# State-space layer: the stores of the turned outputs issued by ScalarE instead of SyncE

## Chip, core and metric

One NeuronCore of a Trainium2 chip runs the whole program. The metric is the device time of one execution in microseconds. TensorE (PE) multiplies matrices, VectorE (DVE), ScalarE (ACT) and GpSimd (POOL) work on tiles, and SyncE (SP) issues transfers. Each engine takes its instructions in the order in which they stand in its own queue, and semaphores tie the engines together. A DMA that an engine issues is an instruction of that queue; the transfer itself runs on 16 DMA engines.

## What is computed

A trunk of two layers over 1024 positions of width 1024, in float32. The first layer mixes attention and a short convolution, the second is a state-space layer, and each is followed by a gated feed-forward network. The change lies in the state-space layer:

```python
def s5_mixer(h, w_in, lambda_re, lambda_im, log_step, b_re, b_im, c_re, c_im, d_skip, w_glu):
    u = (h @ w_in).astype(f32)
    ug = u.reshape(bsz, seq, SSM_GROUPS, SSM_GROUP)        # 64 groups of 16 channels
    ...
    _, _, st_r, st_i = lax.associative_scan(_ssm_combine, (a_r, a_i, bu_r, bu_i), axis=1)
    y = (einsum("gcp,bsgp->bsgc", c_re, st_r) - einsum("gcp,bsgp->bsgc", c_im, st_i)).reshape(...)
    y = y + d_skip * u
    g = jax.nn.gelu(y)
    a, b = jnp.split(g @ w_glu, 2, axis=-1)
    return a * jax.nn.sigmoid(b)
```

## The kernel before

Activations lie with channels on the partitions. Every large matrix product splits both factors in a high and a low part (`wh`, `wl`; `g_h`, `g_l`) and adds three products (`mm_unit`, L169). ScalarE makes the high part of a weight, GpSimd the low part (`split_w`, L150); for G, ScalarE makes the high part and VectorE the low part (`split_g`, L1344).

The state-space layer works in eight blocks m of 128 channels, which are eight groups of 16. Positions are taken as 128 chunks of 8. A block passes through these stages, each a function that is named in the table `order` (L1399):

- U `unit` (L1365): the input product on TensorE. W `weights` splits its weights. E `enter` evicts it as `u`.
- X `store_inputs` (L1249) stores `u` to memory (`ud`), and T `turn_inputs` (L1252) loads it with eight DMAs as `ut`, where a partition holds a position in its chunk and a channel, and the free axis the groups and chunks. The turn is done by way of memory.
- S_ `states` (L1277), one per block, here called step m: `px` on TensorE (L1288), a copy `xs` on ScalarE (L1293, L1294), products and a scan on VectorE (`sc`, L1303), a copy `ss` on ScalarE (L1306, L1307), and `sp` on VectorE. C `copy_rotations` (L1269) copies the rotation table `cs` on ScalarE ahead of it. The step then loads the tables `et` and `cs` of the next one.
- O `emit` (L1318): `py` on TensorE, and GELU on ScalarE into `gy` (L1330). There is one `gy` buffer for blocks 0 to 6; block 7 has another. It then loads the tables `tt` and `co` of the next block.
- R `turn_outputs` (L1334): eight DMAs (L1337) of 16 partitions and 64 KB each store `gy` to `gd`, turned back. F `fetch` loads a block of `gd` as `graw` (L1341), and Q `place` splits it into `g_h` and `g_l`.
- G `gated`: the first three units of the product with `w_glu`, in parts, as blocks of G come in.

All this is recorded under `tc.manual_schedule()` (L1409): the instructions stand in each engine's queue in the order of the table. For the change it matters what stands next to R there:

```python
(C, 1), (S_, 1), (T, 3), (U, 5, 0), (O, 0), (X, 4), (R, 0), (W, 6), (C, 2), (S_, 2), ...
(C, 4), (S_, 4), (R, 2), (F, 1), (X, 6), (C, 5), (S_, 5), ...
(S_, 7), (F, 4), (G, 1, 2, 3), (R, 5), (G, 0, 3, 4), (O, 6), (G, 1, 3, 4), (R, 6), (F, 5), (Q, 4), ...
```

Each DMA counts on one of eight semaphores, and one that uses a semaphore again waits until the transfer that used it last has landed. Before the change all DMAs of the kernel are issued by SyncE. After the stretch the rest of the product with `w_glu`, the second feed-forward network and its last product run.

Of the kernel before, what the change touches and what calls it, by code (L numbers as in the profile page):

```python
# [39 lines left out]
GC = 16  # L40
# [10 lines left out]
def hybrid_trunk_kernel(ctx: ExitStack, tc: tile.TileContext, xt, gains, mix_w_in, w_uq, w_ukv, q_gain, k_gain,  # L51
                        mix_w_out, ssm_w_in, lambda_re, lambda_im, log_step, b_re, b_im, c_re, c_im, d_skip, w_glu,
                        ffn_w_up, ffn_w_down, rope_cos, rope_sin, causal, eye16, halves, out, dbg=None):
    nc = tc.nc
# [216 lines left out]
    for gr in range(2):  # L271
        gts = []
        for i in range(2):
            m = 2 * gr + i
# [959 lines left out]
    gd = dp.tile([KT, P, L, NCH], F32, name="gd")  # L1234
    with ExitStack() as p5s:
# [98 lines left out]
        def turn_outputs(m):  # L1334
            gy = gys.pop(m)
            for j in range(L):
                nc.sync.dma_start(out=gd[m, :, j, :].rearrange("(g c) n -> c g n", c=GC), in_=gy[GC * j:GC * j + GC])  # L1337

        def load_g(m):
            t = wh_tile("graw", F32)  # L1340
# [51 lines left out]
        def place(m):  # L1392
            split_g(m, graw.pop(m))

        pg = []
        U, E, X, T, S_, O, R, W = (unit, into, store_inputs, turn_inputs, step_states, step_outputs, turn_outputs,
                                   weights)
        G, F, Q, C = gated, fetch, place, copy_rotations
# [474 lines left out]
```

## Time and profile before

| | |
|---|---|
| median of 3 runs | 2347.11 us (2344.19 to 2349.64) |
| the profiled execution's own time | 2344.66 us |
| its span | 2342.9 us |
| busy: PE, DVE, ACT, POOL | 2248.5, 1614.7, 851.3, 767.0 us |
| mean granted TensorE clock | 0.986 |
| DMA: one queue, issued by SP | 26.9% of 16 engines' span |
| stores of `gy` | 64 issues of 64 KB, 1370.5 to 1483.1 us, 3.0 us to landing in the median |

The span is the time between the first and the last instruction of the one execution that was profiled. A row of an order of time gives the start, the duration, and in brackets how long the engine was idle before it and whose end ended that. Issues of DMAs do not count as busy time. SPq and ACTq are the queues of SyncE and ScalarE, with their DMA issues and semaphore instructions.

### The profile page before, as it was taken

The page shows a single profiled execution, that of the slowest core. Times are in us where ns is not written, and L with a number is a line of the kernel's source. Part 1 is how long each engine was busy: PE and PEld are TensorE (multiplying, and loading weights), DVE is VectorE, ACT ScalarE, POOL GpSimd, SP SyncE. Part 2 cuts the span into 40 slices and gives each one's busy share as a digit, 9 for nine tenths or more (in the row PEclk, how much of TensorE's full clock was granted, in tenths as well). Part 3 has the DMA queues.
Part 4 walks back from the last instruction along what each step waited for, and adds up shares of the span by engine and source line. Part 5 has one row for each costly group of instructions (what it writes and reads, how often), then busy time and mean ns, then how long its engine had stood idle before and what let it go on. Part 6 is the DMA issues. An engine that isn't in the chain of part 4 may idle for free.

```text
span 2342.9 us, 29810 instructions
## 1 busy us (share of the span) xinstructions
PE 2248.5 (96%) x11228; PEld 1867.9 (80%) x11228; DVE 1614.7 (69%) x2650; ACT 851.3 (36%) x1446; POOL 767.0 (33%) x575
## 2 busy tenths in 40 slices
PE   7999899999999999999999988999789999999999
PEld 6888888888788878888888877788568888878887
DVE  6344677787978778879777487323888888876542
ACT  4112566664232333332223255312444444443110
POOL 4322454435233222232224344431043333324220
PEclk9999999999999999999999998999999999999999
DMA  4112000012122221223332288521132222245301
GB/s 155 45 38 57 1 10 10 10 46 72 29 66 62 82 68 49 76 80 92 101 102 63 93 223 242 171 72 41 54 110 93 82 81 81 81 153 181 125 10 72
DMA packets 227152, 192.04 MB, mean 82 GB/s; under 512 B 25472, under 2 KB 202944, under 8 KB 227008
## 3 DMA queue, kind: packets, MB, share of 16 engines
q1 hardware_dynamic: 227008, 190.14, 26.9%
q8 instruction: 88, 1.44, 0.2%
q14 instruction: 56, 0.46, 0.1%
HBM read 148.22 MB, written 46.07 MB: 83 GB/s over the span
## 4 chain that ended last, share of the span: by engine, by line
PE 79%; DVE 11%; issue 3%; DMA 3%; ACT 3%; POOL 1%; SPq 0%; DVEq 0%; POOLq 0%; ACTq 0%
PE pu L175 31%; PE pd L190 22%; PE pc L1648 4%; PE pb L1648 4%; PE pa L1648 4%; PE pd L1648 2%; PE pu L1554 1%; PE pss L586 1%; PE po L634 1%; PE pckv L378 1%; PE pq L446 1%; PE ptp L615 1%; DVE xT L1696 1%; PE pcq L378 1%; PE pda L644 1%
## 5 line engine op out<-in xcount | busy, mean ns | idle before, releaser
L154 POOL TENSOR_TENSOR wl<-raw,wh 128x1024 fp32r<-128x1024 f32 (+2 forms) x115 | 289.1, 2515 | 487.3 <-ACT wh L153 242.3
L193 DVE TENSOR_TENSOR xT<-pd,xT 128x512 f32<-128x512 f32 x320 | 204.3, 682 | 160.4 <-PE pd L190 159.8
L153 ACT ACTIVATE wh<-raw 128x1024 fp32r<-128x1024 f32 (+2 forms) x117 | 122.4, 1051 | 305.8 <-PE pu L175 212.6
L175 PE MATMUL pu<-f_h,wh 128*128 128x512 f32 x704 | 219.4, 393 | 0.0
L175 PE MATMUL pu<-f_l,wh 128*128 128x512 f32 x704 | 217.2, 390 | 0.0
L175 PE MATMUL pu<-f_h,wl 128*128 128x512 f32 x704 | 216.7, 389 | 0.0
L175 PEld LDWEIGHTS pu<-f_l,wh 128*128 128x128 f32 x704 | 132.1, 188 | 27.9
L175 PEld LDWEIGHTS pu<-f_h,wl 128*128 128x128 f32 x704 | 132.1, 188 | 27.9
L175 PEld LDWEIGHTS pu<-f_h,wh 128*128 128x128 f32 x704 | 130.7, 188 | 28.7 <-issue 1.7
L810 POOL TENSOR_TENSOR gl<-c,gh 128x512 fp32r<-128x512 f32 x44 | 61.4, 1415 | 247.0 <-ACT gh L809 247.0
L1696 DVE SCALAR_TENSOR_TENSOR xT<-u,vec,xT 128x1024 f32<-128x1024 f32 x84 | 111.1, 1330 | 13.3 <-ACT xT L1694 12.6
L759 DVE TENSOR_TENSOR u<-pu,f_rb 128x512 f32<-128x512 f32 x88 | 56.8, 685 | 89.9 <-PE pu L175 87.9
L190 PE MATMUL pd<-gh,wh 128*128 128x512 f32 x352 | 113.5, 403 | 5.4 <-DVE u L759 2.9
L190 PE MATMUL pd<-gh,dwh 128*128 128x512 f32 x352 | 108.8, 390 | 2.5 <-DVE xT L193 1.5
L190 PE MATMUL pd<-gl,wh 128*128 128x512 f32 x352 | 110.4, 395 | 0.0
L190 PE MATMUL pd<-gh,wl 128*128 128x512 f32 x352 | 110.0, 394 | 0.0
L190 PE MATMUL pd<-gh,dwl 128*128 128x512 f32 x352 | 108.5, 389 | 0.0
L190 PE MATMUL pd<-gl,dwh 128*128 128x512 f32 x352 | 108.4, 389 | 0.0
L1796 POOL TENSOR_TENSOR dwl<-raw,dwh 128x1024 fp32r<-128x1024 f32 x20 | 60.8, 3066 | 112.5 <-PE pd L190 84.3
L761 ACT ACTIVATE c<-u,vec 128x512 f32<-128x512 f32 x88 | 59.9, 717 | 69.5 <-DVE u L759 69.1
L190 PEld LDWEIGHTS pd<-gh,wh 128*128 128x128 f32 x352 | 65.8, 191 | 22.6 <-DVE xT L193 4.0
L190 PEld LDWEIGHTS pd<-gh,dwh 128*128 128x128 f32 x352 | 66.1, 188 | 16.9 <-DVE xT L193 1.9
(569 smaller groups left out, 5790.6 us busy)
## 6 DMA issues: line engine op xcount, KB each, us to landing
raw<-in_ffn_w_up_dram SPq DMA_DIRECT2D x50, 512.0 KB, 3.8
raw<-in_ffn_w_down_dram SPq DMA_DIRECT2D x42, 512.0 KB, 4.4
xT<-in_ffn_w_up_dram SPq DMA_DIRECT2D x40, 512.0 KB, 3.6
gfd<-xT SPq DMA_DIRECT2D x21, 512.0 KB, 2.6
raw<-gfd SPq DMA_DIRECT2D x20, 512.0 KB, 4.0
raw<-in_w_glu_dram SPq DMA_DIRECT2D x16, 512.0 KB, 4.0
raw<-in_mix_w_in_dram SPq DMA_DIRECT2D x14, 512.0 KB, 3.9
xT<-in_xt_dram SPq DMA_DIRECT2D x8, 512.0 KB, 7.6
```

The source lines that it names most:

```text
L153: nc.scalar.activation(h[:, 0:n], raw[:, 0:n], AF.Copy)
L154: eng.tensor_tensor(out=l[:, 0:n], in0=raw[:, 0:n], in1=h[:, 0:n].bitcast(F32), op=ALU.subtract)
L175: nc.tensor.matmul(ps[hf], lhsT=w[wi][:, P * k:P * k + P], rhs=xs[k][xi][:, HALVES[hf]], start=(k == 0 and wi == 0 and xi == 0), stop=(k = ...
L190: nc.tensor.matmul(ps[hf], lhsT=ws[i][wi][:, P * f:P * f + P], rhs=gts[i][xi][:, HALVES[hf]], start=(i == first and wi == 0 and xi == 0), ...
L193: nc.vector.tensor_tensor(out=xT[f][:, HALVES[hf]], in0=ps[hf], in1=xT[f][:, HALVES[hf]], op=ALU.add)
L378: nc.tensor.matmul(ps[:, HALF * j:HALF * j + n], lhsT=xa[k][xi][:, P * (2 * p + j):P * (2 * p + j) + P], rhs=w[k // kw][wi][:, n * (k % kw ...
L759: nc.vector.tensor_tensor(out=u[:, 2:HALF + 2], in0=ps[hf], in1=rb[:, HALVES[hf]], op=ALU.mult)
L761: nc.scalar.activation(c, u[:, 2:HALF + 2], AF.Copy, scale=cwcol(layer, 2, m))
L810: nc.gpsimd.tensor_tensor(out=gl[:, cols], in0=cv[hf], in1=gh[:, cols].bitcast(F32), op=ALU.subtract)
L1648: nc.tensor.matmul(ps, lhsT=w[:, HALF * wi + P * k:HALF * wi + P * k + P], rhs=x.at(xi, k), start=(start and k == 0 and wi == 0 and xi == ...
L1696: nc.vector.scalar_tensor_tensor(out=c, in0=u[:, w:S + w], scalar=cwcol(self.layer, w, m), in1=c, op0=ALU.mult, op1=ALU.add)
L1796: eng.tensor_tensor(out=l, in0=raw, in1=h.bitcast(F32), op=ALU.subtract)
```

## The change

`turn_outputs` issues its eight DMAs from ScalarE. Nothing else of the source differs.

```diff
         def turn_outputs(m):
             gy = gys.pop(m)
             for j in range(L):
-                nc.sync.dma_start(out=gd[m, :, j, :].rearrange("(g c) n -> c g n", c=GC), in_=gy[GC * j:GC * j + GC])
+                nc.scalar.dma_start(out=gd[m, :, j, :].rearrange("(g c) n -> c g n", c=GC), in_=gy[GC * j:GC * j + GC])
```

ScalarE's queue at two places: behind `gy` of block 0, and from the second `ss` of step 7 to `g_h` of block 4 and on. `g_h_13966`, `g_h_14013` and `g_h_14023` are `g_h` of blocks 4, 5 and 6.

```order
 L1330 ACT_TABLE_LOAD
 L1330 ACTIVATE gy<-py 128x512 x2
+L1337 DMA gd<-gy 16x8x128 x8
 L153 ACTIVATE wh<-raw 128x1024
 L1269 ACTIVATE cs<-cs 64x2048
```

```order
 L1306 ACTIVATE ss<-sc 64x512
 L1307 ACTIVATE ss<-sc 64x512
+L1337 DMA gd<-gy 16x8x128 x8
 L1330 ACTIVATE gy<-py 128x512 x2
+L1337 DMA gd<-gy 16x8x128 x8
 L1346 ACTIVATE g_h_13966<-graw 128x1024
 L1330 ACTIVATE gy<-py 128x512 x2
+L1337 DMA gd<-gy 16x8x128 x8
 L1346 ACTIVATE g_h_14013<-graw 128x1024
 L1346 ACTIVATE g_h_14023<-graw 128x1024
```

The eight issues stand ahead of `wh` and `cs` at the first place, and ahead of `gy`, `g_h` of block 4 and `g_h` of block 5 at the second. The same instructions leave SyncE's queue.

ScalarE's queue of the changed kernel around R(1), with the semaphores that each instruction waits for (DMAHW0 to DMAHW7 are those of the transfers, and every row's name ends in one number that is the same for all):

```order
L1330 ACTIVATE gy_13238<-py_13249 128x512 [waits PE_49]
L1337 DMA gd_12586<-gy_13238 16x8x128 [waits DMAHW6_49,Activation_49]
L1337 DMA gd_12586<-gy_13238 16x8x128 [waits DMAHW7_49]
L1337 DMA gd_12586<-gy_13238 16x8x128 [waits DMAHW1_49]
L1337 DMA gd_12586<-gy_13238 16x8x128 [waits DMAHW3_49]
L1337 DMA gd_12586<-gy_13238 16x8x128 [waits DMAHW5_49]
L1337 DMA gd_12586<-gy_13238 16x8x128 [waits DMAHW7_49]
L1337 DMA gd_12586<-gy_13238 16x8x128 [waits DMAHW1_49]
L1337 DMA gd_12586<-gy_13238 16x8x128 [waits DMAHW3_49]
L153 ACTIVATE wh_13298<-raw_13146 128x1024
```

On SyncE the eight semaphores were used in turn. Now the two queues share them, and within R(1) numbers 7, 1 and 3 come twice, four issues apart. In R(0) the third issue waits for DMAHW1, on which the load of `co` just ahead of it counts. The first `gy` of block 6, behind R(5), waits for the transfers of R(5):

```order
L1337 DMA gd_12586<-gy_13803 16x8x128 [waits DMAHW4_49]
L1330 ACTIVATE gy_13925<-py_13926 128x512 [waits DMAHW3_49,DMAHW4_49,DMAHW2_49,DMAHW6_49,DMAHW1_49,DMAHW7_49,DMAHW0_49,PE_49]
L1330 ACTIVATE gy_13925<-py_13936 128x512 [waits PE_49]
```

TensorE's queue differs at one place, where the last block of G (`g_h7`) comes in: matmuls of the next unit with blocks 0 and 1 stood ahead of those with block 7, and now stand behind them.

```order
-L175 MATMUL pu_14137<-g_h0_13634,wh_14133 128x512
-L175 MATMUL pu_14138<-g_h0_13634,wh_14133 128x512
-L175 MATMUL pu_14137<-g_l0_13635,wh_14133 128x512
-L175 MATMUL pu_14138<-g_l0_13635,wh_14133 128x512
-L175 MATMUL pu_14137<-g_h0_13634,wl_14134 128x512
-L175 MATMUL pu_14138<-g_h0_13634,wl_14134 128x512
-L175 MATMUL pu_14137<-g_h1_13638,wh_14133 128x512
 L175 MATMUL pu_13691<-g_h7_14059,wh_13579 128x512
 L175 MATMUL pu_13692<-g_h7_14059,wh_13579 128x512
-L175 MATMUL pu_14138<-g_h1_13638,wh_14133 128x512
-L175 MATMUL pu_14137<-g_l1_13639,wh_14133 128x512
-L175 MATMUL pu_14138<-g_l1_13639,wh_14133 128x512
```

Ten matmuls move in this way. VectorE's queue is the same.

## Rows read from the trace of the kernel before

**Rows 1.** The page: chain that ended last, shares of the span by engine.
```profile
PE 79%; DVE 11%; issue 3%; DMA 3%; ACT 3%; POOL 1%; SPq 0%; DVEq 0%; POOLq 0%; ACTq 0%
```

**Rows 2.** Busy time of PE, PEld, DVE, ACT, POOL; granted clock, DMA share, GB/s.
```profile
1340.00:1495.00 155.00, 130.53 (x717) 112.28 (x716) 106.33 (x162) 78.76 (x105) 63.76 (x40) 0.91 0.82 230
...
1495.00:1620.00 125.00, 125.00 (x553) 103.46 (x553) 32.98 (x24) 27.68 (x40) 43.02 (x22) 1.00 0.23 72
```

**Rows 3.** Order of time, PE: start, us, instruction, idle before it and its releaser.
```profile
1371.50 1.20 PE L175 MATMUL pu<-s_h,wh 128*128 128x512 f32 x2 [5.01 <-ACT wh L153]
...
1411.88 3.75 PE L1288 MATMUL px<-ut,et 128*128 128x128 f32 x16 [9.38 <-DMA gd<-gy]
...
1469.91 0.73 PE L175 MATMUL pu<-g_h,wh 128*128 128x512 f32 x2 [3.40 <-ACT g_h L1346]
...
1483.22 0.62 PE L175 MATMUL pu<-g_h,wh 128*128 128x512 f32 x2
...
1492.30 0.97 PE L175 MATMUL pu<-g_h,wh 128*128 128x512 f32 x3 [0.54 <-ACT g_h L1346]
```

**Rows 4.** Order of time, ACT, from the first `gy` to the end of the stretch.
```profile
1369.42 1.08 ACT L1330 ACTIVATE gy<-py 128x512 f32<-128x512 f32 x2
...
1390.83 0.59 ACT L1293 ACTIVATE xs<-px 64x512 f32<-64x512 f32 x1 [2.86 <-PE px L1288]
...
1412.85 0.63 ACT L1306 ACTIVATE ss<-sc 64x512 f32<-64x512 f32 x1 [1.80 <-DVE sc L1303]
...
1427.09 1.07 ACT L1330 ACTIVATE gy<-py 128x512 f32<-128x512 f32 x2
...
1432.50 1.06 ACT L153 ACTIVATE wh<-raw 128x1024 fp32r<-128x1024 f32 x1 [2.45 <-DVE g_l L1347]
1436.58 1.06 ACT L1346 ACTIVATE g_h<-graw 128x1024 fp32r<-128x1024 f32 x1 [3.02 <-DMA graw<-gd]
1437.54 1.07 ACT L1330 ACTIVATE gy<-py 128x512 f32<-128x512 f32 x2
...
1455.74 1.92 ACT L1269 ACTIVATE cs<-cs 64x2048 f32<-64x2048 f32 x1 [1.59 <-DMA cs<-csd]
...
1467.83 1.09 ACT L1330 ACTIVATE gy<-py 128x512 f32<-128x512 f32 x2
1468.80 1.06 ACT L1346 ACTIVATE g_h<-graw 128x1024 fp32r<-128x1024 f32 x1
...
1479.81 2.00 ACT L1346 ACTIVATE g_h<-graw 128x1024 fp32r<-128x1024 f32 x2
```

**Rows 5.** Order of time, SP; then all issues of L1337: ns min/median/max.
```profile
1367.07 0.38 SPq L1274 DMA_DIRECT2D co<-cpd  x1
...
1370.53 3.66 SPq L1337 DMA_DIRECT2D gd<-gy  x8
...
L1337 SPq DMA_DIRECT2D gd<-gy x64: 302/428/997, 1370.5 to 1483.1; - x64
```

**Rows 6.** Issues to landing (us): R(0), R(6), `co` (1367.07), `et` of steps 5, 7.
```profile
gd<-gy SPq DMA_DIRECT2D x8, 64.0 KB, 2.8
...
gd<-gy SPq DMA_DIRECT2D x8, 64.0 KB, 2.1
...
co<-cpd SPq DMA_DIRECT2D x1, 512.0 KB, 5.4
...
et<-etd SPq DMA_DIRECT2D x1, 512.0 KB, 8.8
...
et<-etd SPq DMA_DIRECT2D x1, 512.0 KB, 4.1
```

**Rows 7.** The chain in order of time around the second `ss` of step 7.
```profile
1466.47 0.02 ACTq L1306
1466.49 0.04 issue
1466.53 0.09 ACT ss L1306
1466.62 0.04 issue
1466.66 0.04 ACTq L1330
```

## The prediction

> **What bounds the kernel now.** I read the chain of work first, then the busy time of the stretch around the change, then each engine's order of time there. TensorE carries the chain [rows 1]. The 64 moved stores all lie in the state-space stretch. There TensorE is busy for 130.53 of 155 us, ScalarE for 78.76 [rows 2]. From 1495 to 1620 us TensorE is busy for 125.00 of 125 us [rows 2], and nothing there can take back lost time: what TensorE loses in the stretch, the kernel loses. Inside it TensorE has four long waits: 5.01 us for the weights `wh`, 9.38 before step 5's `px`, 3.40 for `g_h` and 0.54 for the last `g_h` [rows 3]. Three of the four end on an instruction of ScalarE, so I look at what stands ahead of those in ScalarE's queue.
>
> **What moves.** I call the eight stores of channel block m R(m). On SyncE eight unhindered issues take 3.66 us (median of all 64: 428 ns) [rows 5]. SyncE loses all 64, or 64 × 0.428 = 27.4 us of issuing; ScalarE gains them. No row shows a DMA issued by ScalarE. The nearest row is the same store on SyncE, and I take it: 3.7 us for a group. Bounds: 0.04 us for one, as ScalarE's queue takes for a semaphore instruction [rows 7], and 1.0 us, the slowest of the 64 [rows 5].
>
> A group is dear where ScalarE has work behind it. Three things hang on it:
> - The issue itself: each group follows `gy` or a step's `ss`, and the next `wh`, `cs`, `xs` or `g_h` stands behind all eight.
> - A semaphore is used again within R(1) after four issues, as the rows of the order show, and so in R(2) to R(4). Landing takes 2.8 us (median of R(0)'s eight) [rows 6], four issues 4 × 0.46 = 1.9, so 0.9 us more.
> - There is one `gy` buffer, and O(m) waits for R(m-1) to land. That binds where R(m-1) stands just ahead of O(m).
>
> **Does ScalarE issue past a waiting `ss`?** The second `ss` of step 7 waits for VectorE's scan. The semaphore instructions of the `gy` behind it run at 1466.66 us, after the wait was released at 1466.47, not in the 1.8 us before [rows 7]. The queue is held at that wait, and R(2) and R(5), which stand behind such an `ss`, begin at the release; only the two `ss` (1.3 us) lie beside them. The Trainium skill ("Perfetto Trace Analysis", the section on VectorE and ScalarE instructions) says that the sequencer fetches on once an instruction is in the wait queue; by that alone both groups would issue earlier, under the scan, and the sum would be 13.2 us instead of 21.0 (second rival). The row speaks against it here.
>
> **The sum**, as the delay of ScalarE's chain, which TensorE meets at the `g_h` it waits for:
> 1. R(0), between `gy` (ends 1370.50) and the `wh` that TensorE already waits for [rows 3, 4]: 3.7. Its third issue uses the semaphore of `co`, which was issued at 1367.07 and took 5.4 us [rows 5, 6]: to 1372.5 instead of 1371.5, 1.0. Delay 4.7.
> 2. R(1): 3.7 + 0.9, less the 2.86 us that ScalarE waits for step 3's `px` [rows 4]; `px` itself is late by term 1, so that wait stays. +1.7, delay 6.4.
> 3. R(2): 3.7 + 0.9, less the 1.3 beside the two `ss` after 1412.85 [rows 4]. +3.3, delay 9.7. TensorE's wait before step 5 is set by `et`, which lands 8.8 us after its issue [rows 6]; it moves by 4.7 only, so ScalarE is the later one.
> 4. R(3) follows block 3's `gy` (ends 1428.16 [rows 4], now 1437.9). The 4.6 us to 1442.5 lie beside two `g_h` and the 2.45 us wait before `wh`, and the 3.02 us wait for `graw` is swallowed. But `gy` of block 4 must wait for R(3) to land: 1442.5 + 2.8 = 1445.3, against 1437.54 before [rows 4]. Delay now 7.8.
> 5. R(4), ahead of `wh` and step 6's `cs` and `xs`: 3.7 + 0.9. Delay 12.4.
> 6. `cs` of step 7 was late by 1.59 us [rows 4]; this wait is swallowed. Delay 10.8.
> 7. R(5) starts at the release (1466.53 [rows 7]). Eight issues 3.7, landing 2.1 (R(6)'s median [rows 6]), and only then `gy` of block 6, which started at 1467.83 [rows 4]: 3.7 + 2.1 - 1.3 = 4.5. Delay 15.3.
> 8. R(6), between that `gy` and `g_h` of block 4 (1468.80), for which TensorE waits [rows 3, 4]: 3.7. Delay 19.0.
> 9. R(7) moves `g_h` of blocks 5 and 6 (1479.81 [rows 4]) back by 3.7. TensorE first reads block 5 at 1483.22 [rows 3], 2.4 us after it is there: 1.3 exposed. The last `g_h` comes no earlier, so these 1.3 us end in the gap that ten filling matmuls fill now; the order puts those behind it, and they still have to run: 10 × 0.226 us (553 in 125.00 us [rows 2]) = 2.3, of which the 0.54 us wait gives some back. +2.0, delay 21.0.
>
> Together 21.0 us. SyncE's gain is priced at nothing beyond the waits swallowed in 4 and 6, since its loads mostly wait for TensorE to free a single buffer (`et`, `tt`, `co`). The half clock that follows TensorE's stalls is left at nothing: the stalls are there already. The profiled execution took 2344.66 us, 2.45 under the median of the runs (2347.11). 2344.66 + 21.0 = 2365.7, from the median 2368.1; I give **2366**.
>
> **Rivals.**
> - *SyncE's relief decides, and it is faster.* Place: loads behind R(2) to R(4) on SyncE. ScalarE is idle for 76 of 155 us [rows 2], room for eight groups of 3.7. If they fell into it, what is left is the gain: the 3.02 and 1.59 us waits of ScalarE for loads [rows 4], and of TensorE's 9.38 us as much as `et` takes too long (8.8 against 4.1 for a later one, 4.7 [rows 6]): 9.3 us, 2335.4. It decides if the groups expose less than 9.3 us. Against it: `et` stands ahead of R(2) in its queue already, and where R(6) comes to stand, `gy` and `g_h` now follow each other without a gap [rows 4]. The Trainium skill ("DMA: Bandwidth & Descriptors", the section on issuing engines) says that issuing from several engines saves only sequencer time, which takes from this rival the `et` part, leaving 2340.0. Chance 0.05.
> - *ScalarE's queue runs past waiting instructions.* Terms 3 and 7 fall away: delay 6.4, at block 4's `gy` 4.5 by its landing, 9.1 after R(4), 7.5, 11.2 after R(6), 13.2: 2357.9. Against it rows 7. Chance 0.14.
> - *An issue is almost free on ScalarE.* At 0.08 us with its gap a group is 0.6 us, but semaphores and landings remain: R(0) 2.3 (to the landing of `co`), R(1) 0.2, R(2) 1.8, at block 4's `gy` 1.4 in all, R(4) 3.1, `cs` -1.6, R(5) 1.4, R(6) 0.6: 4.9 us, 2349.6, on the edge of what counts as the same. Chance 0.10.
> - *An issue is dearer there.* At 0.8 us a group takes 6.7. Then the semaphores come free by themselves, and the same walk gives 7.0, 10.8, 16.2, 16.3, 23.0, 21.4, 29.0, 35.7, 40.1: 2385. For it: 997 ns in rows 5, and two engines issuing at once. Chance 0.14.
> - *Nothing is seen*, because TensorE waits elsewhere as long. Against it: its waits end on ScalarE. 2345, chance 0.02.
>
> **How the numbers follow.** The forecast has 0.55. It and the run-ahead rival lie in 2352 to 2381, with most of the dear one; almost free, nothing and faster lie below, the worst of dear above: about 0.8 inside. 0.2% is 4.7 us, about what a measurement of this kernel can tell from no change. Slower: 0.55 + 0.14 + 0.14 + half of the almost free case, 0.88. Same: the other half and the nothing case, 0.07. Faster 0.05.
>
> **What would show it.** Step by step: L1337 on ScalarE's queue at about 0.43 us each; `wh` behind R(0) late by about 4.7 us and TensorE's 5.01 us wait near 9; `xs` of step 5 some 10 us late; R(5) directly after the release and `gy` of block 6 after its landing; a TensorE wait of about 10 us for `g_h` of block 4, where there were 3.40. After it TensorE is busy throughout, some 21 us later. The forecast is wrong if an issue costs under 0.1 us, if R(2) and R(5) run during the scan, or if step 5's `px` comes early enough to pay for the rest.

## The result and the profile after

The changed kernel takes 2372.02 us (median of 5 runs, 2370.10 to 2373.57), the kernel before 2347.11 us (5 runs beside them): ratio 1.0107, 95% interval 1.0094 to 1.0121, **24.9 us slower**. The forecast was 2366 us, with a range of 2352 to 2381. The profiled execution of the changed kernel is the slowest of its five (2373.57 us, span 2371.8), so between the two traces the difference is 28.9 us.

The page of the changed kernel, its chain by engine and its two large DMA queues (packets, MB, share of 16 engines' span):

```profile
PE 78%; DVE 11%; issue 3%; ACT 3%; DMA 3%; POOL 2%; ACTq 0%; SPq 0%; DVEq 0%; POOLq 0%
...
q1 hardware_dynamic: 217792, 185.94, 25.8%
q10 hardware_dynamic: 9216, 4.20, 0.7%
```

TensorE carries the chain as before [rows 1], and the stores now have a queue of their own. The busy time by stretch of the changed kernel, with the columns of [rows 2]:

```profile
1340.00:1522.00 182.00, 134.99 (x708) 115.30 (x707) 106.50 (x162) 80.80 (x107) 65.30 (x40) 0.83 0.70 196
1522.00:1647.00 125.00, 125.00 (x553) 103.52 (x552) 30.67 (x23) 25.74 (x38) 40.90 (x21) 1.00 0.22 70
```

The stretch that took 155 us takes 182, with nearly the same counts of instructions on every engine. After it TensorE is busy throughout, as before: nothing is taken back. The granted clock of the stretch fell from 0.91 to 0.83, that is, more of it ran at 1.2 instead of 2.4 GHz, and TensorE's busy time rose by 4.46 us (130.53 to 134.99).

The issues of L1337 (ns min/median/max) in the changed kernel:

```profile
L1337 ACTq DMA_DIRECT2D gd<-gy x64: 309/442/2027, 1370.6 to 1509.3; - x64
```

An issue costs ScalarE 442 ns in the median, about what it cost SyncE, 428 [rows 5]. Its order of time on TensorE, with the columns of [rows 3]:

```profile
1375.51 1.22 PE L175 MATMUL pu<-s_h,wh 128*128 128x512 f32 x2 [8.91 <-ACT wh L153]
...
1422.40 3.75 PE L1288 MATMUL px<-ut,et 128*128 128x128 f32 x16 [11.21 <-DMA cs<-csd]
...
1498.33 1.22 PE L175 MATMUL pu<-g_h,wh 128*128 128x512 f32 x2 [12.98 <-ACT g_h L1346]
...
1510.87 0.74 PE L175 MATMUL pu<-g_h,wh 128*128 128x512 f32 x2 [1.42 <-ACT g_h L1346]
```

The waits of 5.01, 9.38 and 3.40 us [rows 3] are now 8.91, 11.21 and 12.98. The last row is a wait that was not there before: 1.42 us for `g_h` of block 5, which stands behind R(7). The wait of 0.54 us for the last `g_h` is gone. Why the waits grew stands in ScalarE's order of time:

```profile
1370.61 3.74 ACTq L1337 DMA_DIRECT2D gd<-gy  x8
1374.40 1.06 ACT L153 ACTIVATE wh<-raw 128x1024 fp32r<-128x1024 f32 x1 [3.82 <-DMA gd<-gy]
...
1389.08 4.77 ACTq L1337 DMA_DIRECT2D gd<-gy  x8
...
1396.90 0.59 ACT L1293 ACTIVATE xs<-px 64x512 f32<-64x512 f32 x1
...
1410.68 1.91 ACT L1269 ACTIVATE cs<-cs 64x2048 f32<-64x2048 f32 x1 [2.52 <-DMA cs<-csd]
...
1421.41 0.63 ACT L1306 ACTIVATE ss<-sc 64x512 f32<-64x512 f32 x1 [1.74 <-DVE sc L1303]
1421.46 0.79 ACTq L1337 DMA_DIRECT2D gd<-gy  x2
...
1422.29 4.71 ACTq L1337 DMA_DIRECT2D gd<-gy  x6
...
1440.13 1.06 ACT L1330 ACTIVATE gy<-py 128x512 f32<-128x512 f32 x2
...
1451.30 1.09 ACT L1330 ACTIVATE gy<-py 128x512 f32<-128x512 f32 x2 [1.16 <-DMA gd<-gy]
1452.42 7.62 ACTq L1337 DMA_DIRECT2D gd<-gy  x8
1460.14 1.06 ACT L153 ACTIVATE wh<-raw 128x1024 fp32r<-128x1024 f32 x1 [7.75 <-DMA gd<-gy]
...
1475.34 1.91 ACT L1269 ACTIVATE cs<-cs 64x2048 f32<-64x2048 f32 x1
...
1492.03 1.09 ACT L1330 ACTIVATE gy<-py 128x512 f32<-128x512 f32 x2 [4.62 <-DMA gd<-gy]
1493.14 4.04 ACTq L1337 DMA_DIRECT2D gd<-gy  x8
1497.22 1.06 ACT L1346 ACTIVATE g_h<-graw 128x1024 fp32r<-128x1024 f32 x1 [4.11 <-issue]
```

Each group of eight stands as a block of 3.7 to 7.6 us between ScalarE's own instructions, and what follows is later by that. Set beside [rows 4], the delay of ScalarE is 6.1 us at `xs` of step 3 (1390.83 to 1396.90), 8.6 at the `ss` ahead of R(2) (1412.85 to 1421.41), 13.0 and 13.8 at `gy` of blocks 3 and 4, 19.6 at `cs` of step 7, 24.2 at `gy` of block 6 and 28.4 at `g_h` of block 4 (1468.80 to 1497.22).

SyncE, relieved of 64 issues, is not earlier but later:

```profile
1359.77 0.69 SPq L1264 DMA_DIRECT2D cs<-csd  x1
1372.66 3.69 SPq L1258 DMA_DIRECT2D ut<-ud  x8
...
1397.39 1.07 SPq L1264 DMA_DIRECT2D cs<-csd  x1
```

Between its first and its second row it issues nothing for 12 us. The eight loads of `ut` (T(3)) go at 1372.66, 2.05 us after the first store of R(0) was issued on ScalarE (1370.61); the stores land in 2.0 us at the least. T(3) stands ahead of R(0) in the table, and yet it waits for R(0). Likewise one load of T(4) goes at 1391.71 only, 2.6 us after the first store of R(1) (1389.08), which took 2.6 us to land. SyncE's waits for stores from 1340 to 1530 us (engine and line, waited for: us in total, times, longest):

```profile
SPq L1341 <- DMA gd<-gy: 32.5, 7, 11.1
...
SPq L1258 <- DMA gd<-gy: 15.3, 3, 10.7
```

L1341 are the loads of `graw`, which read what the stores write; they waited 1.1 us before the change. L1258 are the `ut` loads, which need no store, and before the change they waited for none. Behind them the `cs` load of the third row of SyncE's order goes 4.8 us later than before (1392.61), and it takes 13.3 us to land instead of 8.5; ScalarE's `cs` of step 4 waits 2.52 us for it. Why it landed more slowly is open. This is a second cost that the forecast does not have, and the last experiments are about it.

### The profile page after: what moved, and what is told of

The parts are those of the page before. It is cut to its first block, busy times and chain, and to the rows that moved or that the text cites. A ratio compares the mean times of both kernels' runs of the same rounds, so it can differ in the third digit from the quotient of the medians.

```text
span 2371.8 us, 29803 instructions
## 1 busy us (share of the span) xinstructions
PE 2257.5 (95%) x11228; PEld 1873.8 (79%) x11228; DVE 1618.5 (68%) x2650; ACT 851.4 (36%) x1446; POOL 766.3 (32%) x575
## 4 chain that ended last, share of the span: by engine, by line
PE 78%; DVE 11%; issue 3%; ACT 3%; DMA 3%; POOL 2%; ACTq 0%; SPq 0%; DVEq 0%; POOLq 0%
PE pu L175 30%; PE pd L190 22%; PE pb L1648 4%; PE pa L1648 4%; PE pc L1648 4%; PE pd L1648 2%; PE pu L1554 1%; PE pss L586 1%; PE po L634 1%; PE pckv L378 1%; DVE xT L1696 1%; PE pq L446 1%; DMA gd<-gy 1%; DVE w L1638 1%; PE ptp L615 1%
## 5 line engine op out<-in xcount | busy, mean ns | idle before, releaser
L1696 DVE SCALAR_TENSOR_TENSOR xT<-u,vec,xT 128x1024 f32<-128x1024 f32 x84 | 112.1, 1341 | 13.3 <-ACT xT L1694 12.6
```

The costliest lines, as they stand in the source:

```text
L1696: nc.vector.scalar_tensor_tensor(out=c, in0=u[:, w:S + w], scalar=cwcol(self.layer, w, m), in1=c, op0=ALU.mult, op1=ALU.add)
```

## Experiments

The theory to begin with was the forecast's: the loss is ScalarE's time, which the issues occupy ahead of work that TensorE waits for. The rival: the two queues hold each other through the eight semaphores, whatever ScalarE does meanwhile. Each run is compared with runs of the kernel before on the same chip. No kernel leaves work out; e1 and e5 add copies to a tile that nothing reads, and e12 adds copies of one column. Where an edit adds or takes lines, the line numbers behind it shift by a few.

### Occupied time alone (e1), and under cover (e5)

e1 is the kernel before, with the stores on SyncE, and six copies on ScalarE at R's places:

```diff
         def turn_outputs(m):
             gy = gys.pop(m)
+            for _ in range(6):
+                nc.scalar.activation(idle, gy[:, 0:4, :], AF.Copy)
```

> The stores stay on SyncE; where the change put eight issues into ScalarE's queue, six copies of 128x512 stand there instead (6 x 0.59 = 3.5 us, written to a tile that nothing reads). Theory (ScalarE's queue is occupied ahead of work that TensorE waits for): most of the loss without a single moved transfer: 3.5 for R(0), 0.7, 3.5, -1.9 at block 4, 3.5, -1.6, 3.5, 3.5 and 2.0 at the end, 17 us, about 2364. Rival (the two queues hold each other up through shared semaphores and shared transfer engines): nothing of that is here, so under 2351.

Measured 2364.65 us beside 2346.14, ratio 1.0072 (1.0057 to 1.0087): **18.5 us** without any DMA on ScalarE. Its order of time on ScalarE shows six copies in 3.94 us, where eight issues take 3.74:

```profile
1369.50 1.08 ACT L1330 ACTIVATE gy<-py 128x512 f32<-128x512 f32 x2
1370.47 3.94 ACT L1337 ACTIVATE idle<-gy 128x512 f32<-128x512 f32 x6
1374.32 1.04 ACT L153 ACTIVATE wh<-raw 128x1024 fp32r<-128x1024 f32 x1
```

So occupied time makes up most of the loss. e5 sets copies of the same length (from a constant tile instead of `gy`) at the places of e4 below: inside the next step, between its `xs` and its `ss`, where ScalarE waits for VectorE's scan.

> Six copies of 128x512 (3.5 us) stand on ScalarE at the places of the run with the stores in the scan's gap; the stores themselves stay on SyncE. This takes the semaphores and the second queue out of that run and leaves the occupied time. Theory (time that lies in ScalarE's gaps costs nothing, and that run lost its 12.8 us by waiting for semaphores that both queues share): 2346 to 2350. Rival (3.5 us in a gap of 3.4 still shift every later step): 2355 to 2360, as with the stores there.

2345.58 us beside 2344.63, ratio 1.0004 (0.9995 to 1.0013): under cover the same 8 × 3.9 us cost nothing. Place, not amount, makes the price.

### One half of the groups (e2, e3)

```diff
-                nc.scalar.dma_start(
+                (nc.scalar if m < 4 else nc.sync).dma_start(
```

> R(0) to R(3) on ScalarE, R(4) to R(7) on SyncE. Theory: the delay of the changed kernel's trace where block 4's gy stands (13.8 less the wait for R(3)), 12.5, less the 1.6 us by which step 7's cs was late: 11 us, 2358. Rival that only the end of the stretch counts (TensorE catches up before): within 2 us of before, 2347 to 2349.

> R(0) to R(3) on SyncE, R(4) to R(7) on ScalarE. Theory: R(4) 4.6 to 8.7, cs of step 7 -1.6, R(5) with its landing 4.5, R(6) 3.7, R(7) 2.0 to 4: 13 to 18 us, 2360 to 2365; e2 and e3 together about the loss of 25 us. Rival that only the end counts: 25 us, 2372.

e2 (R(0) to R(3) on ScalarE): 2356.97 us beside 2346.14, ratio 1.0038 (1.0025 to 1.0052), 10.8 us. e3 (R(4) to R(7), with the two engines exchanged in the line above): 2361.49, ratio 1.0059 (1.0042 to 1.0077), 15.4 us. Both are as expected, and together they are 26.2 against 24.9: within the noise the halves add up. R(4) is dear again in e3, though no earlier group is on ScalarE there:

```profile
1438.68 8.65 ACTq L1337 DMA_DIRECT2D gd<-gy  x8
```

### The issues under cover (e4)

The changed kernel, with R(0), R(1), R(2), R(4) and R(5) recorded inside the next step, behind its `xs` (R(6) stands behind `g_h` of block 4):

```diff
-        def states(m):
+        def states(m, hook=lambda: None):
...
+            hook()
             for hf in both:
                 nc.vector.tensor_tensor(out=z[hf], in0=z[hf], in1=xs[hf], op=ALU.add)
```

> All stores on ScalarE, but R(0), R(1), R(2), R(4) and R(5) are issued inside the next step, between xs and ss, where ScalarE waits 3.4 us for VectorE's scan, and R(6) behind g_h of block 4. Theory (occupied queue): the issues are covered, R(7) alone costs 2 us; 2344 to 2351. Rival (semaphores and transfers shared by two queues): as many issues on ScalarE, so most of the loss stays, 2360 or more.

2358.98 us, ratio 1.0049 (1.0029 to 1.0069): 12.8 us remain, where e5 shows that occupied time costs nothing at these places. That is between the two stated bounds, next to the rival's. ScalarE's order of time, from the third issue of R(1) on:

```profile
1392.65 10.70 ACTq L1338 DMA_DIRECT2D gd<-gy  x6
1403.45 0.63 ACT L1307 ACTIVATE ss<-sc 64x512 f32<-64x512 f32 x1 [10.27 <-DMA gd<-gy]
```

Six issues take 10.70 us, and the `ss` behind them is late. Two of them are long by themselves (2.05 and 0.71 us; why is open). The last four take again the numbers of the group's first four, by the order of the built program, and wait until those have landed: SyncE's DMAs take turns in the dealing, and the group gets only four of the eight numbers. So the rival has a share too, and the theory of occupied time alone falls.

### One store per block (e6, e7)

To take the occupied time out, `gd` is laid out so that one DMA of 128 partitions stores a block, and SyncE turns it with eight loads in F. e6 issues the store from ScalarE; e7 differs only in `nc.sync` for `nc.scalar`:

```diff
-    gd = dp.tile([KT, P, L, NCH], F32, name="gd")
+    gd = dp.tile([KT, 8, P, NCH], F32, name="gd")
...
-            for j in range(L):
-                nc.scalar.dma_start(out=gd[m, :, j, :].rearrange("(g c) n -> c g n", c=GC), in_=gy[GC * j:GC * j + GC])
+            nc.scalar.dma_start(out=gd[m].rearrange("g q n -> q g n"), in_=gy)
...
-            nc.sync.dma_start(out=t, in_=gd[m].rearrange("p j n -> p (j n)"))
+            tv = t.rearrange("p (j n) -> p j n", j=L)
+            for g in range(8):
+                nc.sync.dma_start(out=tv[GC * g:GC * g + GC], in_=gd[m, g].rearrange("(j c) n -> c j n", c=GC))
```

> gd is laid out so that a block is stored by one DMA of 128 partitions (ScalarE) and loaded back by eight of 16 (SyncE). ScalarE issues 8 instead of 64. Theory (occupied queue): 0.45 us where there were 3.7, and few semaphores used twice; what is left is the landing ahead of block 6's gy (3 us) and later loads of graw: 2347 to 2355. Rival (the cost is the transfers' own, moved to a second queue): as many bytes there, 2365 or more.

> The control of the run before: the same layout, both the store and the eight loads on SyncE. Theory: SyncE issues as much as in the kernel before, only the loads come some 3 us later: 2345 to 2351. If the layout itself costs, this run shows how much: then 2352 or more, and the run with ScalarE is read against it.

e7: 2346.88 us beside 2344.63, ratio 1.0007 (0.9997 to 1.0016); the layout costs nothing that can be told. e6: 2378.36, ratio 1.0145 (1.0130 to 1.0160), **33.7 us slower** with eight issues on ScalarE that take 3 us in all, worse than the change with 64. The expectation missed by far. SyncE's order of time in e6, then two rows of ScalarE's:

```profile
1361.57 13.41 SPq L1258 DMA_DIRECT2D ut<-ud  x8
...
1407.15 13.95 SPq L1342 DMA_DIRECT2D graw<-gd  x8
```

```profile
1417.40 0.37 ACTq L1336 DMA_DIRECT2D gd<-gy  x1
...
1431.40 1.91 ACT L1269 ACTIVATE cs<-cs 64x2048 f32<-64x2048 f32 x1 [12.78 <-DMA cs<-csd]
```

The eight loads of T(3) take 5.09 us in e7 and 13.41 here. ScalarE issues R(2) at 1417.40 only, behind the `ss` of step 4, and SyncE's loads stand still about then; ScalarE waits 12.78 us for `cs`.

### Earlier stores, more buffers (e8 to e11)

Four runs asked whether late stores, or single terms of the forecast, carry the loss. e8 is the changed kernel with `(R, 6)` moved behind `(Q, 4)` in the table, e11 the changed kernel with `bufs=2` for `gy`. e9 is e6, and e10 the changed kernel, with R(2), R(3) and R(5) directly behind their O.

> The changed kernel, but R(6) stands behind g_h of block 4 in ScalarE's queue, not ahead of it. Theory: TensorE's wait of 13.0 us for that g_h shrinks by the 4.1 us that R(6) took: 2368. Rival (TensorE waits there for something else that is as late, such as the load of graw): within 1.5 us of the changed kernel, 2371 to 2373.

> The changed kernel with two gy buffers in place of one, so that the gelu of a block no longer waits for the landing of the block before it (waits of 1.16, 4.62 and about 1 us at blocks 4, 6 and 7 in the changed kernel's order of time). By the forecast's terms for the landing (2.1 us at R(5), 1.2 at block 4) it gains 3 to 5 us: 2367 to 2369. If what is saved is given back at the semaphores of the next group, as it was in e8, it stays at 2370 to 2374.

> The changed kernel (64 issues by ScalarE, 2372.0 us) with the stores of blocks 2, 3 and 5 set directly behind their gy. If the loss is mostly ScalarE's occupied queue (3.7 us in the way of the next step wherever the group stands behind gy), it stays: 2367 to 2374. If late stores of ScalarE that hold SyncE's loads carry a large part of it (some 7 us beyond the 18 of occupation), it falls to 2362 to 2367.

e8: 2372.88 us, ratio 1.0120 (1.0104 to 1.0135). e11: 2370.90, ratio 1.0114 (1.0097 to 1.0131). e10: 2372.11, ratio 1.0123 (1.0104 to 1.0142). None gains what can be told. In e8 the moved group gave what the forecast's term says: TensorE's wait for `g_h` of block 4 fell from 12.98 to 9.62 us. But R(7) then took 6.89 us instead of 3.70, and the next wait for `g_h` grew:

```profile
1489.82 1.22 PE L175 MATMUL pu<-g_h,wh 128*128 128x512 f32 x2 [9.62 <-ACT g_h L1346]
...
1506.36 1.22 PE L175 MATMUL pu<-g_h,wh 128*128 128x512 f32 x2 [4.58 <-ACT g_h L1346]
```

Here the saving was given back at the next group. Whether the same holds in e10 and e11 is not shown.

> As e6 (one store per block, issued by ScalarE, 2378.4 us), with the stores of blocks 2, 3 and 5 set directly behind their gy. If e6's loss came from ScalarE issuing its stores late (R(2) at 1417.40, behind the ss of step 4), with SyncE's loads held behind them on the shared semaphores, most of it goes: the eight issues themselves take 8 x 0.37 = 2.9 us of ScalarE, so 2347 to 2358 us, and PE's wait of 20.35 us for et of step 5 is gone. If the loss came from the form of the store or from a second queue as such, it stays within 6 us of 2378.

e9: 2367.57 us beside 2344.28, ratio 1.0094 (1.0073 to 1.0116). It is 10.8 us better than e6, so the late stores were part of it, but 23.3 us remain, between the two bounds that were stated. SyncE's order of time over two short stretches, then from the view of the DMAs the landing of R(0) (count, size, us from issue to landing):

```profile
1362.12 1.74 SPq L1258 DMA_DIRECT2D ut<-ud  x4
...
1373.73 1.72 SPq L1258 DMA_DIRECT2D ut<-ud  x4
```

```profile
gd<-gy ACTq DMA_DIRECT2D x1, 512.0 KB, 2.9
```

ScalarE issues R(0) at 1370.77, directly behind `gy`. Four loads of T(3) go at once; the fifth goes at 1373.73, and 1370.77 + 2.9 = 1373.7: when R(0) has landed. The order of the built program tells why. These are the first five of SyncE's eight loads of T(3), and R(0) on ScalarE (the number in front is a place in the engine's own queue):

```text
417 L1258 DMA ut<-ud 16x8x128 [waits DMAHW6_49,DMAHW1_49]
418 L1258 DMA ut<-ud 16x8x128 [waits DMAHW2_49]
419 L1258 DMA ut<-ud 16x8x128 [waits DMAHW3_49]
420 L1258 DMA ut<-ud 16x8x128 [waits DMAHW4_49]
421 L1258 DMA ut<-ud 16x8x128 [waits DMAHW5_49]
...
804 L1336 DMA gd<-gy 128x8x128 [waits DMAHW5_49,Activation_49]
```

The built program deals out the semaphores in one order for both queues, in turn, and in that order R(0) comes ahead of T(3), though the table has T(3) first. R(0) took number 5, and the fifth load has to wait until R(0) has given it back. On one queue (e7) the numbers follow that queue's own order, in which T(3) stands ahead of R(0). The wait is one that nothing in the data asks for.

### The numbers in another order (e12)

If that is so, e9 must lose most of its 23.3 us when the numbering changes. e12 makes ScalarE read one column of the `ut` tile ahead of the store, so that R(0) is dealt its number after T(3). The copy also makes the store wait for `ut`, which by itself can only hold it up:

```diff
         def turn_outputs(m):
             gy = gys.pop(m)
+            t = {0: 3, 1: 4, 2: 5, 3: 6, 5: 7}.get(m)
+            if t is not None:
+                nc.scalar.activation(seen[:, t:t + 1], inputs[t][:, 0, 0:1], AF.Copy)
```

> As e9 (2367.6 us), but ahead of five of its eight stores ScalarE copies one column (128x1) of the ut tile that SyncE loads for step m+3 (step 7 for block 5). The tile was there long before in e7, so by the trace nothing is waited for that was late; but the built program then numbers ScalarE's store behind those loads, and no longer ahead of them, so that the store takes a semaphore after SyncE's eight loads have taken theirs. Theory (what cost e9 23 us is SyncE's loads that stood behind ScalarE's later stores in the round of eight semaphores; T(3)'s fifth load went at 1373.73, 10 us behind the fourth, once R(0) had landed): most of it goes, 2346 to 2354 us, and T(3)'s eight loads go out within 5 us from about 1362. Rival (a second queue, or stores beside loads, cost that time themselves): it stays within 5 us of 2367.

2352.35 us beside 2344.51, ratio 1.0041 (1.0027 to 1.0054): 7.8 us instead of 23.3, within the bounds of the theory and far from the rival's. SyncE's T(3), then ScalarE's copy and store, in order of time:

```profile
1358.24 4.74 SPq L1258 DMA_DIRECT2D ut<-ud  x8
```

```profile
1366.83 0.20 ACT L1338 ACTIVATE seen<-ut 128x1 f32<-128x1 f32 x1
1366.97 0.39 ACTq L1339 DMA_DIRECT2D gd<-gy  x1
```

All eight loads go within 4.74 us, ahead of the store, and the store itself goes 3.8 us earlier than in e9 (1370.77). Adding work to ScalarE made the kernel 15 us faster. SyncE's waits for `gd<-gy` from 1340 to 1530 us, first in e9, then in e12 (engine and line, waited for: us in total, times, longest):

```profile
SPq L1258 <- DMA gd<-gy: 26.7, 4, 12.0
SPq L1342 <- DMA gd<-gy: 24.5, 4, 9.9
```

```profile
SPq L1345 <- DMA gd<-gy: 19.7, 4, 6.6
...
SPq L1258 <- DMA gd<-gy: 6.1, 1, 6.1
```

The waits of `ut` loads for stores fell from 26.7 to 6.1 us. What the last 7.8 us are is open. ScalarE's copies themselves wait, 1.56 us at the tile of step 4 and 2.51 at that of step 5, and the loads of `graw` (L1345) still wait 19.7 us for stores, some of it because they load what those stores write. The changed kernel itself with its numbering put right was not run.

No version tried is faster than the kernel before.

## Why the prediction was right, step by step

The sign, the range and the main mechanism held: 2372.0 in 2352 to 2381, 6.0 us above the forecast. Some 2 of the 6.0 us come from the base, since the forecast adds its 21.0 us to the profiled execution's 2344.66; in the medians the loss is 24.9. Between the traces, term by term (us added to the delay, worked out from the rows of both; term 9 is what is left of the whole):

| term | forecast | measured |
|---|---|---|
| 1 R(0) | 4.7 | 4.0 (TensorE's wait ends 1371.50, 1375.51) |
| 2 R(1) | 1.7 | 2.1 |
| `cs` of step 4 late | none | 2.5 |
| 3 R(2) | 3.3 | 4.5 |
| 4 R(3), to `gy` of block 4 | -1.9 | 0.7 |
| 5 R(4) | 4.6 | 7.4 |
| 6 `cs` of step 7 | -1.6 | -1.6 |
| 7 R(5) and its landing | 4.5 | 4.6 |
| 8 R(6) | 3.7 | 4.2 |
| 9 R(7), to the end | 2.0 | 0.5 |
| sum | 21.0 | 28.9 (24.9 in the medians) |

Terms 1 and 9 were too high by 0.7 and 1.5 us, which by luck hid part of what the others lacked.

- **The price of an issue** was right: 442 ns for the 428 taken, 3.74 us for the first group against 3.7. Its wait of 1.0 us for the semaphore of `co` (term 1) did not come. That number had last been taken by a load of T(2), by the built program's order; the section on the change and the forecast took it for the load of `co` just ahead.
- **R(2) and R(5) start at the release.** R(2)'s first issue is at 1421.46, 0.05 us after the second `ss` starts; its first two issues run beside `ss`, none in the 1.74 us before it. R(5) begins in the same way, at 1486.20 beside the second `ss` of step 7. The rival by which the queue runs past waiting instructions is out. The Trainium skill ("Perfetto Trace Analysis", the section on VectorE and ScalarE instructions) has the sequencer free for the next instruction as soon as one is in the wait queue. The rows on `ss`, here and in [rows 7], do not test that, as the forecast took them to: what waits for the scan there is a semaphore instruction of its own just ahead of `ss` (`ACTq L1306` in [rows 7]). Two other rows do, the second `gy` of block 7, which itself waits for TensorE, and the four semaphore instructions that stand ahead of groups of R (with the first and the last start):

```profile
1505.39 0.60 ACT L1330 ACTIVATE gy<-py 128x512 f32<-128x512 f32 x1 [1.19 <-PE py L1328]
...
L1337 ACTq EVENT_SEMAPHORE  x4: 17/17/17, 1367.1 to 1505.4; - x4
```

The last of the four stands directly behind that `gy` in the queue, and it ran when `gy` started, at 1505.4, not in the 1.19 us before; so the trace does not agree with that page. The first, at 1367.1, ran ahead of a table load and the two `gy` of block 0 (1369.50) that stand before it, and whose `py` TensorE had finished at 1364.8. In these rows the queue runs past instructions that wait for ScalarE itself, but not past one that waits for another engine.

- **Terms 6, 7 and 8** came as worked out: the 1.59 us wait for `cs` [rows 4] is gone, `gy` of block 6 waits 4.62 us for the landing of R(5), and TensorE's 3.40 us wait [rows 3] became 12.98 ("about 10"). In term 9 the wait that opens is 1.42 us for the 1.3 worked out; the price of the ten moved matmuls did not show.
- **The step that failed** is "SyncE's gain is priced at nothing beyond the waits swallowed", which let it only gain or stay. It lost: held behind ScalarE's stores on the shared semaphores, SyncE issued the `cs` load of step 4 4.8 us later, and with its slower landing (13.3 us for 8.5) `cs` came 2.5 us late, which no term had. The order rows ahead of the prediction show that the two queues share the eight numbers; the forecast priced that on ScalarE's side alone (0.9 us in a group).
- **Term 5 was mis-sized by its landing.** R(4) takes 7.62 us instead of 4.6 (8.65 in e3). These are its first and its last four issues, and the landing of the first four:

```profile
1452.42 1.84 ACTq L1337 DMA_DIRECT2D gd<-gy  x4
...
1457.79 2.25 ACTq L1337 DMA_DIRECT2D gd<-gy  x4
...
gd<-gy ACTq DMA_DIRECT2D x4, 64.0 KB, 5.8
```

In the dealing R(4) alternates with SyncE's DMAs, most of them loads of T(7), so its last four issues take the numbers of its first four, and between them ScalarE stands still for 3.5 us. The forecast had this wait, but sized it with a landing of 2.8 us (R(0)'s median). With 5.8 in its place its own sum gives 3.7 + 5.8 - 1.9 = 7.6 (4 × 0.46 is 1.84, which changes this by less than 0.1). Why these stores landed so late is open. Terms 3 and 4 are off in the same direction, by 1.2 and 2.6 us; R(2) has the longest issue of all, 2.03 us, and its cause is open too.

- **The clock** was left at nothing, since "the stalls are there already". They grew, and TensorE's busy time in the stretch grew by 4.46 us. How much of that lies on the chain no run tells; e1 has some of it too (0.88 granted from 1340 to 1513 us).
- **SyncE's relief**, the rival by which it would be faster, is out: the kernel is slower, and no run gained from the relief.

By the runs, 18.5 of the 24.9 us are occupied time of ScalarE (e1); the other 6.4, by difference, are semaphores and landings. The two causes are shown one at a time (e1 without DMAs, e9 and e12 with almost no occupied time); that they share the loss in just that proportion in the changed kernel is worked out, not shown. The shares do not simply add: with the occupied time under cover (e4) 12.8 us remain, and 18.5 + 12.8 is more than 24.9.

## What to carry to other kernels

A DMA issue occupies the engine that issues it, here 442 ns in the median: read the price at each place from what stands behind it in the queue. A place where the engine waits for another anyway takes away the price of the time (e5), but not that of the semaphores (e4). Before a DMA goes to a second queue, read in the built program in which order the two queues are dealt their semaphores: a load that shares a number with a store of the other queue, dealt earlier, waits for that store even if it stands far ahead of it in the code. Look at the relieved engine's waits too, and not only at the loaded one's.

## What the runs showed of the hardware that was not expected

- Eight issues of 0.37 us on a second queue cost 33.7 us (e6), and 64 issues of 0.44 us cost 24.9: what counts is not the number of issues, but where they stand and when they give their semaphores back.
- Five added copies of 0.20 us took 15 us away (e9 to e12). The Trainium skill ("DMA: Bandwidth & Descriptors", "Issuing engines are not separate DMA queues") says that issuing on several engines at once only saves the sequencer's time for it. The runs agree so far as none is faster than the kernel before. Whether the transfers themselves changed they do not separate: the stores land in 2.3 us in the median instead of 3.0, in a stretch that moved 196 GB/s instead of 230 [rows 2]. The cost through semaphores, 33.7 and 23.3 us in e6 and e9, is of the size of the 64 × 0.428 = 27.4 us of issuing that SyncE saved in the changed kernel.
